# Interleaving the two token halves in the activations, so that stationary operands are read with a step of two columns

## The chip, the cores and the metric

The kernel runs on one core of a Trainium2 chip. The metric is the device time of one execution in microseconds, as the median of several runs. TensorE does the matrix products: a load (LDWEIGHTS) puts a stationary operand of up to 128 x 128 numbers in place, and a matmul then streams a moving operand of up to 512 columns past it and adds the result into an accumulator in PSUM. VectorE and ScalarE work on what comes out, DMA queues bring the weights from memory. Each engine works through its own queue of instructions, and they wait for each other by semaphores.

## The reference

256 tokens with 2048 features go through two transformer-like blocks in float32. What matters here is that nearly all of the work is products of activations with weight matrices:

```python
proj = h @ w_in[i]
...
merged = (jax.nn.sigmoid(gate_sb) * (y_sb @ w_sb_out[i])
          + jax.nn.sigmoid(gate_ca) * (y_ca @ w_ca_out[i]))
x = x + merged @ w_mix_out[i]
h = rmsnorm(x, g_ffn[i])
g_ff, u_ff = jnp.split(h @ w_ffn_in[i], 2, axis=-1)
x = x + (jax.nn.silu(g_ff) * u_ff) @ w_ffn_out[i]
...
x = x + jax.nn.sigmoid(h @ w_ple_gate[i]) * (p[i] @ w_ple_in[i])
```

The first block has two attention branches, a feed-forward part with 5632 hidden features and a gated addition. The second block has a state-space branch, a gated linear attention, a differential attention, and a feed-forward part with 5504 hidden features and a short convolution over the tokens.

## The kernel before

Every float32 operand of a large product is split into a high part in the format fp32r and a low part, the rest. A product is then three products: low by high, high by low and high by high, accumulated in the same place. The weights are split as they arrive (`high`, a cast on ScalarE, L485; `low`, a subtraction on VectorE, L495) into one long tile `W`, some halves ahead of their use.

An activation is held feature-major in an `Acts` object: in slots of [128 features, 4, 512], where the 512 columns of one group of 128 features are first the high parts of tokens 0 to 255 and then their low parts. `at(k)` gives the 512 columns of group k, `two(k)` those of two groups. The splitting is done by `hilo` (L317): ScalarE writes the high part (L320, or L312 with a scale), VectorE the low part (L321, or L315 with a scale). It is called wherever activations are made: at the start from the transposed input, in `to_acts` after TensorE's transposes (L348), in `yt_out` and `head_norm` for the heads of the attentions, in `hidden1` and `hidden2` of the feed-forward parts, in `ple_start`, and at the end of the state-space branch `s5`.

A list of jobs is worked off in order by `stream`; each job is a chain of halves, and a half is one weight transfer of 512 KB. There are two kinds that matter:

- Token-major jobs (`AS`, in `mm_as`): the stationary operand is 128 tokens of an activation's high or low part, the moving operand 512 columns of a weight. For each group of features and each half m of the tokens there are three matmuls: L583 (low activation, high weight), L584 (high activation, low weight), L585 (high, high). Each has a load of its own. The result is [128 tokens, 2 halves, 512].
- Feature-major jobs (`WS`): the stationary operand is a 128 x 128 piece of a weight, the moving operand an activation. L545 streams all 512 columns (high and low tokens) past the weight's high part, L549 the 256 high columns past its low part. The result holds, for 128 output features, 256 columns of one kind and 256 of the other, and `ws_sum` (L441) adds the two: a copy on ScalarE (L444), an addition on VectorE (L445), and where a row norm is to be applied a product on VectorE (L447).

A third kind (`W4`, one job) streams an activation past 32 columns of a weight at a time (L538). The first half of all is worked off with the low weights last (`low_last`, L573 to L576), because they arrive last.

Between the halves, `tick` lets generators advance that issue the work on the other engines, so the order of instructions on each engine is fixed when the kernel is built.

Of the kernel before, what the change touches and what calls it, by code (L numbers as in the profile page):

```python
# [168 lines left out]
class Acts:  # L169


    def __init__(self, n):
        self.n, self.slots, self.ready = n, {}, set()

    def at(self, k):
        return self.slots[k // 4][0][:, k % 4, :]

    def two(self, k):
        return self.slots[k // 4][0][:, k % 4:k % 4 + 2, :]


class Job:
# [5 lines left out]
class Build:  # L188
# [127 lines left out]

    def hilo(self, hi, lo, src, scale=None):  # L317

        if scale is None:
            self.nc.scalar.copy(hi, src)  # L320
            self.nc.vector.tensor_sub(lo, src, hi.bitcast(F32))  # L321
        else:
            self.act(hi, src, AF.Copy, scale=scale)
            self.stt(lo, src, scale, ALU.mult, hi.bitcast(F32), ALU.subtract)


    def open_acts(self, acts, g):
# [11 lines left out]
    def to_acts(self, src, acts, n, scale=None, gcol=None):  # L339

        yield from self.open_acts(acts, n)
        banks = []
        for half in range(2):
            b = yield from self.bank()
            for kk in range(2):
                for m in range(2):
                    c = half * 256 + kk * 128
                    self.nc.tensor.transpose(b[0][:, kk * 256 + m * 128:kk * 256 + m * 128 + 128],  # L348
                                             src[:, m, c:c + 128], self.ident)
            banks.append(b)  # L350
        yield
        for half in range(2):
            k = 4 * n + 2 * half
            if gcol is None:
                t = acts.two(k)
                ps = banks[half][0].rearrange("p (k t) -> p k t", k=2)
                self.hilo(t[:, :, 0:256], t[:, :, 256:512], ps, scale)
            else:
                for kk in range(2):
                    t = acts.at(k + kk)  # L360
                    self.hilo(t[:, 0:256], t[:, 256:512], banks[half][0][:, kk * 256:kk * 256 + 256],
                              self.par[:, gcol + k + kk:gcol + k + kk + 1])
            acts.ready.update((k, k + 1))
            self.unbank(banks[half])
# [76 lines left out]
    def ws_sum(self, acc, out, rb=None, n=2):  # L441

        nc = self.nc
        nc.scalar.copy(out, acc[:, 0:n, 256:512])  # L444
        nc.vector.tensor_add(out, acc[:, 0:n, 0:256], out)  # L445
        if rb is not None:
            nc.vector.tensor_mul(out, out, rb.tile[:, None, :].to_broadcast([128, n, 256]) if n > 1 else  # L447
                                 rb.tile[:, None, :])


    def stream(self, jobs):
# [56 lines left out]
        for i, (j, idx, ks) in enumerate(halves):  # L508
# [23 lines left out]
            if j.kind == "AS":  # L532
                self.mm_as(j.acts, ks, wh, wl, acc, (0, 1), first, end, low_last=i == 0)
            elif j.kind == "W4":

                for k in range(16):
                    p = slice(32 * (k % 4), 32 * (k % 4) + 32)
                    nc.tensor.matmul(acc[p, 0, :], lhsT=wh[:, 32 * k:32 * k + 32],  # L538
                                     rhs=j.acts.at(k).bitcast(F32), start=k < 4, stop=k >= 12)
            else:  # L540
                for kk, k in enumerate(ks):
                    x = j.acts.at(k)
                    for f in range(2):
                        s = slice((kk * 2 + f) * 128, (kk * 2 + f) * 128 + 128)
                        hi = lambda: nc.tensor.matmul(  # L545
                            acc[:, f, :], lhsT=wh[:, s], rhs=x, start=k == first, stop=k == end)
                        if k == first:
                            hi()
                        nc.tensor.matmul(acc[:, f, 256:512], lhsT=wl[:, s], rhs=x[:, 0:256], start=False, stop=False)  # L549
                        if k != first:  # L550
                            hi()
# [10 lines left out]
    def mm_as(self, acts, ks, wh, wl, acc, ms, first, end, low_last=False):  # L562

        nc = self.nc
        if low_last:
            for low in (False, True):
                for kk, k in enumerate(ks):
                    s = slice(kk * 512, kk * 512 + 512)
                    for m in ms:
                        x = acts.at(k)  # L570
                        xh, xl = x[:, m * 128:m * 128 + 128], x[:, 256 + m * 128:384 + m * 128]
                        if low:
                            nc.tensor.matmul(acc[:, m, :], lhsT=xh, rhs=wl[:, s], start=False, stop=False)  # L573
                        else:
                            nc.tensor.matmul(acc[:, m, :], lhsT=xl, rhs=wh[:, s], start=k == first, stop=False)
                            nc.tensor.matmul(acc[:, m, :], lhsT=xh, rhs=wh[:, s], start=False, stop=False)  # L576
            return
        for kk, k in enumerate(ks):
            x = acts.at(k)
            s = slice(kk * 512, kk * 512 + 512)  # L580
            for m in ms:
                xh, xl = x[:, m * 128:m * 128 + 128], x[:, 256 + m * 128:384 + m * 128]
                nc.tensor.matmul(acc[:, m, :], lhsT=xl, rhs=wh[:, s], start=k == first, stop=False)  # L583
                nc.tensor.matmul(acc[:, m, :], lhsT=xh, rhs=wl[:, s], start=False, stop=False)  # L584
                nc.tensor.matmul(acc[:, m, :], lhsT=xh, rhs=wh[:, s], start=False, stop=k == end)  # L585
# [38 lines left out]
    def first(self):  # L624
# [6 lines left out]
        def start(load):  # L631
# [10 lines left out]
            for k in range(16):  # L642
# [4 lines left out]
                    tri = self.more_consts("tri", 256, nc.sync)  # L647
                    self.U, self.msb = tri[:, 0:128], tri[:, 128:256]
                yield from self.open_acts(XT, k // 4)
                t = XT.at(k)  # L650
                self.hilo(t[:, 0:256], t[:, 256:512], xs[k // 8][0][:, k % 8, :], self.col(P_GMIX + k))
                XT.ready.add(k)
                if k % 2:
                    yield
# [41 lines left out]
        def yt_out(Y, h, b, key):  # L696

            yield from self.open_acts(Y, h // 4)
            t = Y.at(h)
            self.hilo(t[:, 0:256], t[:, 256:512], b[0][:, 0:256])  # L700
            Y.ready.add(h)
            self.unbank(b)
            Y.left -= 1
# [157 lines left out]
        def ple_start():  # L861
# [3 lines left out]
            s = self.slot([128, 2, 256])  # L865
            nc.gpsimd.dma_start(out=s[0], in_=d["pt"])
            PT.slots[0] = self.slot([128, 4, 512], F32R)
            t = PT.two(0)
            self.hilo(t[:, :, 0:256], t[:, :, 256:512], s[0])
            self.drop(s)  # L870
            PT.ready.update((0, 1))

# [87 lines left out]
    def hidden1(self, j, kl, acc, free, hid, rb):  # L960
# [8 lines left out]
        self.act(s[:, 0], s[:, 0], AF.Silu)  # L969
        v.tensor_mul(s[:, 0], s[:, 0], s[:, 1])  # L970
        yield
        t = hid.at(kl)
        self.hilo(t[:, 0:256], t[:, 256:512], s[:, 0])
        hid.ready.add(kl)

    def ffn(self, wu, wd, nf, acts, rb, hidden, fin):
# [419 lines left out]
    def head_norm(self, b, t, w, acts, h, post):  # L1396
# [20 lines left out]
        for vh in range(2):  # L1417
# [6 lines left out]
        dst = acts.two(2 * h)  # L1424
        self.hilo(dst[:, :, 0:256], dst[:, :, 256:512], t.rearrange("p (a t) -> p a t", a=2))
        acts.ready.update((2 * h, 2 * h + 1))
        yield

    def hidden2(self, j, kl, acc, free, hid, rb):
# [17 lines left out]
        self.act(c[:, 1], c[:, 1], AF.Silu)  # L1447
        v.tensor_mul(c[:, 0], c[:, 0], c[:, 1])
        yield
        h = hid.at(kl)  # L1450
        self.hilo(h[:, 0:256], h[:, 256:512], c[:, 0])
        hid.ready.add(kl)


# [203 lines left out]
    def s5(self, uslot, ZT):  # L1658
# [61 lines left out]
        for j2 in range(4):  # L1720
# [33 lines left out]
            if j2 % 2:  # L1754
# [5 lines left out]
                t = ZT.slots[g][0]  # L1760
                yield

                for jj in range(4):
                    yt = y[:, jj].rearrange("p (t c) -> p c t", t=4)
                    hi, lo = (t[:, jj, h:h + 256].rearrange("p (c t) -> p c t", t=4) for h in (0, 256))
                    self.hilo(hi, lo, yt)
                    if jj % 2:
                        yield
# [25 lines left out]
```

## Time and profile before

| | |
|---|---|
| median of 3 runs | 3138.79 us (3138.43 to 3139.48) |
| the profiled execution, whole | 3139.36 us |
| its span, from the first to the last instruction | 3137.6 us |
| mean granted TensorE clock | 0.999 |
| data moved by DMA | 618 MB, 197 GB/s in the mean |

The rows of the profile that matter stand in the prediction. A row of a group names the line, the engine, the operation, what it writes and reads, its shape and its count; behind the first bar are the busy time in us and the mean duration of one in ns, behind the second the engine's idle time before such instructions, and what ended it. A row of the timeline begins with the start and the duration in us. PE is TensorE's matmuls, PEld its loads of stationary operands, DVE is VectorE, ACT is ScalarE. Matmuls overlap: a matmul's duration is longer than the distance to the next one's start.

### The profile page before, as it was taken

To read this page: it belongs to the slowest core of one execution; us is meant where nothing else is said; L and a number is where in the kernel's file an instruction comes from. 1 tells how busy PE (TensorE), PEld (TensorE's weight loads), DVE (VectorE), ACT (ScalarE), POOL (GpSimd) and SP (SyncE) were. 2 spreads that over 40 slices of the span, in tenths; PEclk is the share of its full clock that TensorE was granted. 3 is DMA by queue.
4 is the path that set the end of the run, shared out by engine and by line. 5 is a ranking of instruction groups with operands and counts; after the bars stand their busy time and mean duration, and the time that the engine had idled before them with its cause. 6 is when DMAs were issued, how large, how long until landed. Compare 5 with 4: busy or idle time off the path is not lost.

```text
span 3137.6 us, 45166 instructions
## 1 busy us (share of the span) xinstructions
PE 3119.9 (99%) x17629; PEld 2651.4 (85%) x17629; DVE 1993.1 (64%) x2593; ACT 1553.3 (50%) x2035; POOL 73.4 (2%) x158
## 2 busy tenths in 40 slices
PE   9999999999999999999999999999999999999998
PEld 7888888888888888888888888888888888888887
DVE  5656445557577677566655667945555766757766
ACT  6544444455444454456544454444445654545545
POOL 0000000000001000000000001000000000000000
PEclk9999999999999999999999999999999999999999
DMA  7554555555667766655654575655555555555554
GB/s 265 170 180 163 189 194 187 182 189 189 216 224 243 255 224 233 198 175 189 216 181 162 174 221 197 211 191 199 200 186 181 190 195 186 191 196 188 192 188 168
DMA packets 172645, 618.00 MB, mean 197 GB/s; under 512 B 23552, under 2 KB 23968, under 8 KB 169232
## 3 DMA queue, kind: packets, MB, share of 16 engines
q1 hardware_dynamic: 164992, 577.49, 55.4%
q0 software_dynamic: 7440, 37.64, 3.5%
q8 instruction: 138, 2.26, 0.3%
q14 instruction: 75, 0.61, 0.1%
HBM read 599.74 MB, written 14.25 MB: 196 GB/s over the span
## 4 chain that ended last, share of the span: by engine, by line
PE 99%; ACT 0%; DMA 0%; DVE 0%; DVEq 0%; issue 0%; SPq 0%; ACTq 0%
PE acc L545 29%; PE acc L583 17%; PE acc L584 17%; PE acc L585 17%; PE acc L549 15%; PE p L348 1%; PE p L1699 0%; PE p L1739 0%; PE p L1156 0%; PE p L930 0%; PE p L931 0%; PE p L932 0%; PE p L1152 0%; PE p L1742 0%; PE p L1133 0%; PE p L1733 0%
## 5 line engine op out<-in xcount | busy, mean ns | idle before, releaser
L495 DVE TENSOR_TENSOR w<-raw,w 128x1024 fp32r<-128x1024 f32 x1088 | 1320.2, 1220 | 644.2 <-PE acc L584 421.7
L485 ACT CAST w<-raw 128x1024 fp32r<-128x1024 f32 x1088 | 1138.4, 1049 | 1092.4 <-PE acc L585 637.3
L545 PE MATMUL acc<-s,w 128*128 128x512 f32 x3936 | 1369.5, 393 | 0.0
L549 PE MATMUL acc<-s,w 128*128 128x256 f32 x3936 | 1090.4, 282 | 0.0
L583 PE MATMUL acc<-w,s 128*128 128x512 f32 x2372 | 932.4, 393 | 0.8 <-DVE big L1376 0.8
L585 PE MATMUL acc<-w,s 128*128 128x512 f32 x2372 | 923.6, 389 | 0.0
L584 PE MATMUL acc<-w,s 128*128 128x512 f32 x2372 | 923.5, 389 | 0.0
L545 PEld LDWEIGHTS acc<-s,w 128*128 128x128 f32 x3936 | 733.4, 188 | 153.5
L549 PEld LDWEIGHTS acc<-s,w 128*128 128x128 f32 x3936 | 740.2, 188 | 10.4 <-issue 1.0
L583 PEld LDWEIGHTS acc<-w,s 128*128 128x128 f32 x2372 | 445.6, 188 | 93.8 <-issue 1.7
L585 PEld LDWEIGHTS acc<-w,s 128*128 128x128 f32 x2372 | 445.3, 188 | 93.5
L584 PEld LDWEIGHTS acc<-w,s 128*128 128x128 f32 x2372 | 445.7, 188 | 90.9 <-issue 0.5
L445 DVE TENSOR_TENSOR s<-acc,s 128x512 f32<-128x512 f32 (+1 forms) x120 | 82.7, 690 | 263.8 <-ACT s L444 263.7
L444 ACT COPY s<-acc 128x512 f32<-128x512 f32 (+1 forms) x120 | 70.1, 585 | 189.1 <-PE acc L545 186.9
L312 ACT ACTIVATE s<-s 128x256 f32<-128x256 f32 (+4 forms) x175 | 76.6, 443 | 105.1 <-DVE s L315 38.0
L315 DVE SCALAR_TENSOR_TENSOR s<-s,conv 128x256 f32<-128x256 f32 x172 | 79.4, 482 | 3.1
L447 DVE TENSOR_TENSOR s<-s,rb 128x512 f32<-128x512 f32 (+1 forms) x104 | 71.7, 689 | 3.5
L320 ACT CAST s<-s 128x256 fp32r<-128x256 f32 (+1 forms) x104 | 45.7, 443 | 30.1 <-DVE s L970 15.0
L1655 DVE TENSOR_TENSOR s<-s,s 128x1024 f32<-128x1024 f32 x48 | 58.5, 1220 | 0.0
L312 ACT ACTIVATE s<-s,conv 128x256 f32<-128x256 f32 x86 | 47.1, 595 | 22.0 <-DVE s L447 22.0
L321 DVE TENSOR_TENSOR s<-s,s 128x256 fp32r<-128x256 f32 (+1 forms) x104 | 47.6, 460 | 15.8 <-ACT s L320 15.8
L312 ACT ACTIVATE junk<-big 128x512 f32<-128x512 f32 x48 | 30.3, 632 | 50.7 <-DVE big L949 32.4
(265 smaller groups left out, 1007.7 us busy)
## 6 DMA issues: line engine op xcount, KB each, us to landing
raw<-in_w_fin SPq DMA_DIRECT2D x176, 512.0 KB, 4.3
raw<-in_w_up SPq DMA_DIRECT2D x172, 512.0 KB, 4.0
raw<-in_w_fout SPq DMA_DIRECT2D x88, 512.0 KB, 4.3
raw<-in_w_down SPq DMA_DIRECT2D x84, 512.0 KB, 4.2
raw<-in_w_qksb SPq DMA_DIRECT2D x32, 512.0 KB, 3.8
raw<-in_w_qkca SPq DMA_DIRECT2D x32, 512.0 KB, 3.5
raw<-in_w_gsb SPq DMA_DIRECT2D x32, 512.0 KB, 3.9
raw<-in_w_gca SPq DMA_DIRECT2D x32, 512.0 KB, 4.2
```

What stands on the lines that cost most here:

```text
L312: self.nc.scalar.activation(out, in_, func, scale=scale, **kw)
L315: self.nc.vector.scalar_tensor_tensor(out=out, in0=in0, scalar=scalar, in1=in1, op0=op0, op1=op1)
L444: nc.scalar.copy(out, acc[:, 0:n, 256:512])
L445: nc.vector.tensor_add(out, acc[:, 0:n, 0:256], out)
L447: nc.vector.tensor_mul(out, out, rb.tile[:, None, :].to_broadcast([128, n, 256]) if n > 1 else rb.tile[:, None, :])
L485: nc.scalar.copy(wh[:, :n], raws[i][:, :n])
L495: nc.vector.tensor_sub(wl[:, :n], r[:, :n], wh[:, :n].bitcast(F32))
L545: hi = lambda: nc.tensor.matmul(acc[:, f, :], lhsT=wh[:, s], rhs=x, start=k == first, stop=k == end)
L549: nc.tensor.matmul(acc[:, f, 256:512], lhsT=wl[:, s], rhs=x[:, 0:256], start=False, stop=False)
L583: nc.tensor.matmul(acc[:, m, :], lhsT=xl, rhs=wh[:, s], start=k == first, stop=False)
L584: nc.tensor.matmul(acc[:, m, :], lhsT=xh, rhs=wl[:, s], start=False, stop=False)
L585: nc.tensor.matmul(acc[:, m, :], lhsT=xh, rhs=wh[:, s], start=False, stop=k == end)
```

## The change

The 256 tokens are stored so that the two halves take turns: token t of half 0, token t of half 1, token t + 1 of half 0, and so on, first for all high parts, then for all low parts. `at(k)` and `two(k)` give two views now, one of the high and one of the low parts, with the indices half m and token t, in which t steps by two columns. `moving(k)` is new and gives the 512 columns as they lie.

- Token-major matmuls take as stationary operand the 128 tokens of a half from these views, so that each load reads every second column. Moving operand, order and number of matmuls stay.
- Feature-major matmuls and the `W4` job stream `moving(k)`, as they lie. Their results' columns then stand in the alternating order, and `ws_sum` reads the accumulator with a step of two and writes the usual order.
- `hilo` writes its two results through the alternating views. Where it is given a scale and two groups at once (`to_acts` with a constant scale), VectorE's part is done in two instructions, one for each group.
- In `s5` the reordering of the tokens at the end goes through the same views.

```diff
 class Acts:
+    def moving(self, k):
+        return self.slots[k // 4][0][:, k % 4, :]
+
     def at(self, k):
-        return self.slots[k // 4][0][:, k % 4, :]
+        v = self.moving(k).rearrange("p (h t m) -> p h m t", h=2, m=2)
+        return v[:, 0], v[:, 1]
 
     def two(self, k):
-        return self.slots[k // 4][0][:, k % 4:k % 4 + 2, :]
+        v = self.slots[k // 4][0][:, k % 4:k % 4 + 2, :].rearrange("p k (h t m) -> p h k m t", h=2, m=2)
+        return v[:, 0], v[:, 1]
...
     def hilo(self, hi, lo, src, scale=None):
+        if len(src.shape) < len(hi.shape):
+            src = src.rearrange("p (m t) -> p m t" if len(src.shape) == 2 else "p k (m t) -> p k m t", m=2)
         if scale is None:
             self.nc.scalar.copy(hi, src)
             self.nc.vector.tensor_sub(lo, src, hi.bitcast(F32))
         else:
             self.act(hi, src, AF.Copy, scale=scale)
-            self.stt(lo, src, scale, ALU.mult, hi.bitcast(F32), ALU.subtract)
+            for k in range(hi.shape[1]) if len(hi.shape) == 4 else (slice(None),):
+                self.stt(lo[:, k], src[:, k], scale, ALU.mult, hi[:, k].bitcast(F32), ALU.subtract)
...
     def ws_sum(self, acc, out, rb=None, n=2):
-        nc.scalar.copy(out, acc[:, 0:n, 256:512])
-        nc.vector.tensor_add(out, acc[:, 0:n, 0:256], out)
+        a = acc[:, 0:n, :].rearrange("p n (h t m) -> p h n m t", h=2, m=2)
+        o = out.rearrange("p n (m t) -> p n m t", m=2)
+        nc.scalar.copy(o, a[:, 1])
+        nc.vector.tensor_add(o, a[:, 0], o)
...
-                    x = j.acts.at(k)
+                    x = j.acts.moving(k)
...
         for kk, k in enumerate(ks):
-            x = acts.at(k)
             s = slice(kk * 512, kk * 512 + 512)
             for m in ms:
-                xh, xl = x[:, m * 128:m * 128 + 128], x[:, 256 + m * 128:384 + m * 128]
+                xh, xl = (x[:, m] for x in acts.at(k))
                 nc.tensor.matmul(acc[:, m, :], lhsT=xl, rhs=wh[:, s], start=k == first, stop=False)
                 nc.tensor.matmul(acc[:, m, :], lhsT=xh, rhs=wl[:, s], start=False, stop=False)
                 nc.tensor.matmul(acc[:, m, :], lhsT=xh, rhs=wh[:, s], start=False, stop=k == end)
...
-                    yt = y[:, jj].rearrange("p (t c) -> p c t", t=4)
-                    hi, lo = (t[:, jj, h:h + 256].rearrange("p (c t) -> p c t", t=4) for h in (0, 256))
+                    yt = y[:, jj].rearrange("p (t m c) -> p m c t", t=4, m=2)
+                    hi, lo = (t.rearrange("p m (c t) -> p m c t", t=4) for t in ZT.at(4 * g + jj))
                     self.hilo(hi, lo, yt)
```

The other places of the diff are calls of `hilo`, which pass `*acts.at(k)` or `*acts.two(k)` in place of two slices.

More of the change, by code (lines that the diff above doesn't have):

```diff
@@ L356, in to_acts @@
                 ps = banks[half][0].rearrange("p (k t) -> p k t", k=2)
-                self.hilo(t[:, :, 0:256], t[:, :, 256:512], ps, scale)
+                self.hilo(*t, ps, scale)
             else:
@@ L360, in to_acts @@
                     t = acts.at(k + kk)
-                    self.hilo(t[:, 0:256], t[:, 256:512], banks[half][0][:, kk * 256:kk * 256 + 256],
+                    self.hilo(*t, banks[half][0][:, kk * 256:kk * 256 + 256],
                               self.par[:, gcol + k + kk:gcol + k + kk + 1])
@@ L538, in stream @@
                     nc.tensor.matmul(acc[p, 0, :], lhsT=wh[:, 32 * k:32 * k + 32],
-                                     rhs=j.acts.at(k).bitcast(F32), start=k < 4, stop=k >= 12)
+                                     rhs=j.acts.moving(k).bitcast(F32), start=k < 4, stop=k >= 12)
             else:
                 for kk, k in enumerate(ks):
-                    x = j.acts.at(k)
+                    x = j.acts.moving(k)
                     for f in range(2):
@@ L578, in mm_as @@
         for kk, k in enumerate(ks):
-            x = acts.at(k)
             s = slice(kk * 512, kk * 512 + 512)
             for m in ms:
-                xh, xl = x[:, m * 128:m * 128 + 128], x[:, 256 + m * 128:384 + m * 128]
+                xh, xl = (x[:, m] for x in acts.at(k))
                 nc.tensor.matmul(acc[:, m, :], lhsT=xl, rhs=wh[:, s], start=k == first, stop=False)
@@ L649, in start @@
                 yield from self.open_acts(XT, k // 4)
-                t = XT.at(k)
-                self.hilo(t[:, 0:256], t[:, 256:512], xs[k // 8][0][:, k % 8, :], self.col(P_GMIX + k))
+                self.hilo(*XT.at(k), xs[k // 8][0][:, k % 8, :], self.col(P_GMIX + k))
                 XT.ready.add(k)
@@ L698, in yt_out @@
             yield from self.open_acts(Y, h // 4)
-            t = Y.at(h)
-            self.hilo(t[:, 0:256], t[:, 256:512], b[0][:, 0:256])
+            self.hilo(*Y.at(h), b[0][:, 0:256])
             Y.ready.add(h)
@@ L867, in ple_start @@
             PT.slots[0] = self.slot([128, 4, 512], F32R)
-            t = PT.two(0)
-            self.hilo(t[:, :, 0:256], t[:, :, 256:512], s[0])
+            self.hilo(*PT.two(0), s[0])
             self.drop(s)
@@ L971, in hidden1 @@
         yield
-        t = hid.at(kl)
-        self.hilo(t[:, 0:256], t[:, 256:512], s[:, 0])
+        self.hilo(*hid.at(kl), s[:, 0])
         hid.ready.add(kl)
@@ L1423, in head_norm @@
                 self.stt(c, c, s1, ALU.mult, s2, ALU.mult)
-        dst = acts.two(2 * h)
-        self.hilo(dst[:, :, 0:256], dst[:, :, 256:512], t.rearrange("p (a t) -> p a t", a=2))
+        self.hilo(*acts.two(2 * h), t.rearrange("p (a t) -> p a t", a=2))
         acts.ready.update((2 * h, 2 * h + 1))
@@ L1449, in hidden2 @@
         yield
-        h = hid.at(kl)
-        self.hilo(h[:, 0:256], h[:, 256:512], c[:, 0])
+        self.hilo(*hid.at(kl), c[:, 0])
         hid.ready.add(kl)
@@ L1759, in s5 @@
                 yield from self.open_acts(ZT, g)
-                t = ZT.slots[g][0]
                 yield
                 for jj in range(4):
-                    yt = y[:, jj].rearrange("p (t c) -> p c t", t=4)
-                    hi, lo = (t[:, jj, h:h + 256].rearrange("p (c t) -> p c t", t=4) for h in (0, 256))
+                    yt = y[:, jj].rearrange("p (t m c) -> p m c t", t=4, m=2)
+                    hi, lo = (t.rearrange("p m (c t) -> p m c t", t=4) for t in ZT.at(4 * g + jj))
                     self.hilo(hi, lo, yt)
```

## The prediction

> **What bounds the kernel now.** I read the page's head first, then its chain, then the costliest groups, and then the timeline, because the groups' durations overlap and do not say how fast matmuls follow each other.
>
> ```profile
> span 3137.6 us, 45166 instructions
> PE 3119.9 (99%) x17629; PEld 2651.4 (85%) x17629; DVE 1993.1 (64%) x2593; ACT 1553.3 (50%) x2035; POOL 73.4 (2%) x158
> ...
> PE 99%; ACT 0%; DMA 0%; DVE 0%; DVEq 0%; issue 0%; SPq 0%; ACTq 0%
> PE acc L545 29%; PE acc L583 17%; PE acc L584 17%; PE acc L585 17%; PE acc L549 15%; PE p L348 1%; PE p L1699 0%; PE p L1739 0%; PE p L1156 0%; PE p L930 0%; PE p L931 0%; PE p L932 0%; PE p L1152 0%; PE p L1742 0%; PE p L1133 0%; PE p L1733 0%
> ```
>
> TensorE is busy for 99% of the span and is 99% of the chain that ended last. The three token-major lines (L583, L584, L585) are 17% each, so about half the span. The other half is the feature-major pair L545 and L549. The list of TensorE's waits has two entries:
>
> ```profile
> PE acc L575 <- ACT w L485: 7.7, 1, 7.7
> PE acc L583 <- DVE big L1376: 0.8, 1, 0.8
> ```
>
> After the start, TensorE waited 0.8 us for anybody. The time is therefore the number of matmuls times the distance from one start to the next. The counts and the loads of the stationary operand:
>
> ```profile
> L583 PE MATMUL acc<-w,s 128*128 128x512 f32 x2372 | 932.4, 393 | 0.8 <-DVE big L1376 0.8
> L585 PE MATMUL acc<-w,s 128*128 128x512 f32 x2372 | 923.6, 389 | 0.0
> L584 PE MATMUL acc<-w,s 128*128 128x512 f32 x2372 | 923.5, 389 | 0.0
> ...
> L585 PEld LDWEIGHTS acc<-w,s 128*128 128x128 f32 x2372 | 445.3, 188 | 93.5
> ```
>
> There are 3 x 2372 = 7116 token-major matmuls of 512 columns, each with a load of its own that takes 188 ns. Their distance, from TensorE's timeline:
>
> ```profile
> 1450.01 0.39 PE L584 MATMUL acc<-w,s 128*128 128x512 f32 x1
> 1450.23 0.39 PE L585 MATMUL acc<-w,s 128*128 128x512 f32 x1
> ...
> 1455.45 0.39 PE L584 MATMUL acc<-w,s 128*128 128x512 f32 x1
> ```
>
> From one L584 to the eighth L584 after it are 24 matmuls: 5.44 us / 24 = 226.7 ns. What 512 columns need at least is seen at the very start, where TensorE still ran slowly (the granted clock reads 1.00 there, so the pace itself is the sign):
>
> ```profile
> 8.30 0.63 PE L576 MATMUL acc<-w,s 128*128 128x512 f32 x1
> ...
> 10.86 0.63 PE L576 MATMUL acc<-w,s 128*128 128x512 f32 x1
> ```
>
> ```profile
> 7.70:13.00 5.30, 5.29 (x13) 1.00 1.03 409
> ```
>
> Six distances in 2.56 us are 426.7 ns each, which I read as exactly half speed: 2 x 213.3. Then 512 columns cost 213.3 ns at full speed, and each of the 7116 matmuls carries **13.3 ns** that is not columns. In all that is 94.9 us. The feature-major pairs carry the same:
>
> ```profile
> 1502.71 0.39 PE L545 MATMUL acc<-s,w 128*128 128x512 f32 x1
> 1502.94 0.28 PE L549 MATMUL acc<-s,w 128*128 128x256 f32 x1
> ...
> 1504.80 0.39 PE L545 MATMUL acc<-s,w 128*128 128x512 f32 x1
> ```
>
> Six pairs in 2.09 us are 348 ns a pair, to the 10 ns of the view; 512 and 256 columns are 320 ns, so some 14 ns remain for each matmul, whether 512 or 256 columns long. At half speed the extra vanished altogether. A fixed step at each change of the stationary operand would be longer at half speed, or as long. Something that fits into the gaps of a slower stream behaves as seen. The transposes are a second case:
>
> ```profile
> 1431.21 1.04 PE L348 MATMUL p<-cst,big 128*128 128x128 f32 x8
> ...
> L348 PE MATMUL p<-cst,big 128*128 128x128 f32 x128 | 16.6, 272 | 0.0
> ```
>
> The last of eight takes about 0.27 of the 1.04 us, so seven distances are 0.77 us, 110 ns each. That is twice as long per column as in a large matmul (106.7 ns for 128 columns), and the extra is some 3 ns. Here too the stream is slower and the extra small. So the 13.3 ns looks like the load and the moving stream getting in each other's way while both read.
>
> **The change, part by part.** *The load.* It keeps 128 columns and its place behind the previous matmul; only its addresses change, from neighbouring words to every second word. How quickly it reads comes from two load rows:
>
> ```profile
> L1699 PEld LDWEIGHTS p<-s,s 128*32 128x32 f32 x512 | 7.5, 110 | 2.6 <-issue 2.0 <-PE acc L584 0.4 <-PE acc L549 0.3
> ```
>
> 188 - 110 = 78 ns for 96 more columns is 0.81 ns a column, against 0.417 ns a column for the moving stream. So today the load walks through memory at half the stream's pace, and the stream sweeps past it again and again. With a step of two the load walks 8 bytes in 0.81 ns, which is the stream's own pace. If the two disturb each other where they hit the same part of memory, as the shrinking extra suggests, then one push apart is enough and they stay apart. No row shows a stationary operand with a step, so this is bounded from both sides. The best end is that all 13.3 ns go: -94.9 us. The bad end is that the load, which covers 1024 bytes in place of 512, disturbs twice as much: 13.3 becomes 26.7 ns, +94.9 us. I take the value of the transposes' row, the nearest in which a load hardly disturbs: an extra of 3.3 ns, a distance of 216.6 ns, 10.0 ns less. 7116 x 10.0 = **-71.2 us**.
>
> *The splitting into high and low parts, and the sums.* `hilo` now writes every second word, and `ws_sum` reads the accumulator with that step. The nearest rows are the splittings of the state-space branch, which read with a step of 64 words, beside plain ones:
>
> ```profile
> L320 ACT CAST s<-s x4: 647/658/668, 2081.5 to 2084.2; 128x256 fp32r<-128x256 f32 x4
> ```
>
> ```profile
> L320 ACT CAST s<-s x5: 404/408/409, 2908.2 to 2952.7; 128x256 fp32r<-128x256 f32 x5
> ```
>
> ```profile
> L321 DVE TENSOR_TENSOR s<-s,s x4: 618/621/637, 2082.2 to 2085.0; 128x256 fp32r<-128x256 f32 x4
> ```
>
> ```profile
> L321 DVE TENSOR_TENSOR s<-s,s x5: 417/420/425, 2909.2 to 2953.7; 128x256 fp32r<-128x256 f32 x5
> ```
>
> For 256 columns that is +250 ns on ScalarE and +201 ns on VectorE; the lower bound is nothing. I keep the dear end. The sums:
>
> ```profile
> L445 DVE TENSOR_TENSOR s<-acc,s 128x512 f32<-128x512 f32 (+1 forms) x120 | 82.7, 690 | 263.8 <-ACT s L444 263.7
> L444 ACT COPY s<-acc 128x512 f32<-128x512 f32 (+1 forms) x120 | 70.1, 585 | 189.1 <-PE acc L545 186.9
> ```
>
> A sum has 512 columns, so +0.40 us on VectorE and +0.50 us on ScalarE. The tightest place is the second feed-forward's feature-major stretch, in which twelve blocks of 11.1 us (32 pairs of 347 ns) follow each other:
>
> ```profile
> 2453.00:2586.00 133.00, 133.00 (x717) 115.09 (x717) 95.44 (x127) 71.24 (x95) 1.02 (x10) 1.00 0.58 193
> ```
>
> VectorE is busy for 95.4 of 133 us (the columns are TensorE, loads, VectorE, ScalarE, GpSimd). Twelve blocks add at most 12 x 0.60 = 7.2 us there, and 12 x 0.75 = 9 us to ScalarE's 71.2. Both stay under 80%, behind TensorE, which covers them. `to_acts` gets one more VectorE instruction per pair where its scale is a constant (16 in all, under 0.5 us each), also covered. What is not covered is the first matmul, which waits 7.7 us at the start behind two ScalarE splittings: +0.5 us at most. I put +1 us for that and for joins. No DMA is added or moved, and no queue or wait is reordered. If the token-major stages run 4% faster, the weights must come 4% faster; DMA is busy for 0.58 of the stretch above, so that has room.
>
> **Sum.** The profiled execution took 3139.4 us (its span 3137.6 and 1.8 around it; the median of the runs shown is 3138.8, 0.6 less). 3139.4 - 71.2 + 1 = **3069 us**. Its own range goes from 3139.4 - 94.9 = 3044 to half the gain, 3104.
>
> **The rivals.** *Nothing moves: 3139 to 3141.* The 13.3 ns may belong to the hand-over between two stationary operands, whatever the addresses. For it speaks that it is the same in both kinds of job; against it, that it is absent at half speed. [...]
>
> *Slower: about 3235.* The place is the same 7116 loads. If a load takes a slot from the moving stream for each piece of memory that it opens, and not where the two happen to meet, then twice the bytes covered is twice the price: 13.3 more ns, +94.9 us. It decides from the first token-major job on. For it speaks that the extra is so constant; against it, only that the stream seems to have gaps at half speed, which both readings allow. At worst the load also gets as slow per column as the stepped ScalarE splitting (+0.98 ns a column): 188 + 125 = 313 ns. In the pairs a load of 188 ns fits behind a distance of some 120 ns, so it may run about 70 ns past its matmul's start; behind 226.7 ns about 298 ns fit. The distance would be 242 ns and the time about 3249. [...]
>
> *VectorE or ScalarE becomes the bound.* At under 80% of the tightest stretch I give this no chance of its own.
>
> **How the numbers follow.** Faster by the likeliest mechanism 0.52, nothing moves 0.19, slower around 3235 0.22, worse than that 0.07. A measurement of this kernel can tell about 0.2% (6 us) from no change: faster 0.52, same 0.19, slower 0.29. The range goes from 3044 to 3237 us. It must reach the slower case, since leaving that out would leave out 0.29.
>
> **What would show it.** Right: L583 to L585 start 215 to 219 ns apart, their loads stay near 188 ns, the pairs stay at 347 ns, and the sums and splittings on ScalarE and VectorE get longer without a wait of TensorE. Distances of 227 ns mean that nothing moves; 240 ns and more mean the slower rival, with load rows still at 188 ns if it takes slots, and near 300 ns if it is slow itself. New waits of TensorE for VectorE or ScalarE, or pairs that change, would make the working wrong in a place that I put at nothing.

## The result and the profile after

The change makes the kernel slower. The median of three runs is 3187.67 us (3187.60 to 3187.93) against 3138.79 us: a ratio of 1.0156, with a 95% interval from 1.0142 to 1.017. Of thirteen further runs of the kernel before, made beside the first experiments, twelve lay between 3138.45 and 3140.01 us and one, at 8091.52 us, is not compared with anything here. The prediction was 3069 us with a range from 3044 to 3237; the time lies in the range, but the likeliest direction, faster, was wrong.

The head of the page of the changed kernel and its chain of waits (the line numbers have moved: L545 is now L557, L549 is L561, and L583, L584, L585 are L593, L594, L595):

```profile
span 3186.0 us, 45182 instructions
PE 3168.1 (99%) x17629; PEld 2696.3 (85%) x17629; DVE 1995.6 (63%) x2609; ACT 1555.9 (49%) x2035; POOL 72.8 (2%) x158
...
PE acc L557 28%; PE acc L593 18%; PE acc L595 17%; PE acc L594 17%; PE acc L561 15%; PE p L358 1%; PE p L1703 0%; PE p L1743 0%; PE p L1162 0%; PE p L937 0%; PE p L939 0%; PE p L938 0%; PE p L1158 0%; PE p L1746 0%; PE p L1139 0%; PE p L1737 0%
```

The list of TensorE's waits has the same two entries as before:

```profile
PE acc L586 <- ACT w L497: 7.8, 1, 7.8
PE acc L593 <- DVE big L1382: 0.8, 1, 0.8
```

So TensorE still sets the time and waits for nobody new. It has the same 17629 matmuls and is busy 48.2 us longer. Which ones take longer is seen in the groups, first of the kernel before, which the prediction did not show, then of the one after:

```profile
L545 PE MATMUL acc<-s,w 128*128 128x512 f32 x3936 | 1369.5, 393 | 0.0
L549 PE MATMUL acc<-s,w 128*128 128x256 f32 x3936 | 1090.4, 282 | 0.0
```

```profile
L557 PE MATMUL acc<-s,w 128*128 128x512 f32 x3936 | 1369.7, 393 | 0.0
L561 PE MATMUL acc<-s,w 128*128 128x256 f32 x3936 | 1090.5, 282 | 0.0
L593 PE MATMUL acc<-w,s 128*128 128x512 f32 x2372 | 946.5, 399 | 0.8 <-DVE big L1382 0.8
L595 PE MATMUL acc<-w,s 128*128 128x512 f32 x2372 | 937.2, 395 | 0.0
...
L595 PEld LDWEIGHTS acc<-w,s 128*128 128x128 f32 x2372 | 459.9, 194 | 96.6
```

The feature-major pairs are unchanged to 0.2 us in 1369 and 0.1 in 1090. The token-major matmuls are some 6 ns longer each (393 to 399, 389 to 395), and so are their loads (188 to 194). The distance from one matmul to the next is what counts, and it stands in TensorE's timeline:

```profile
1472.34 0.39 PE L595 MATMUL acc<-w,s 128*128 128x512 f32 x1
...
1477.94 0.40 PE L595 MATMUL acc<-w,s 128*128 128x512 f32 x1
```

From one L595 to the eighth after it are 24 matmuls: 5.60 us / 24 = 233.3 ns, where it was 226.7. With 213.3 ns for the columns, the extra of each matmul went from 13.3 to **20.0 ns**. 7116 x 6.67 ns = 47.4 us, which is nearly all of the 48.4 us by which the span grew. (Summed over the whole trace, each matmul from its start to the next one's, the token-major matmuls take 48.5 us more and the feature-major ones 0.2 us.) At the very start, where the pace was read as half speed, the distance is still that of before:

```profile
8.39 0.63 PE L587 MATMUL acc<-w,s 128*128 128x512 f32 x1
...
10.95 0.63 PE L587 MATMUL acc<-w,s 128*128 128x512 f32 x1
```

Six distances in 2.56 us are 426.7 ns each, as before the change: at that pace the stepped load adds nothing.

The work beside TensorE, the splittings from 2900 to 3100 us and the groups of the sums:

```profile
L329 ACT CAST s<-s x12: 417/433/437, 2909.1 to 3098.6; 128x256 fp32r<-128x256 f32 x12
```

```profile
L330 DVE TENSOR_TENSOR s<-s,s x12: 416/418/422, 2910.2 to 3099.6; 128x256 fp32r<-128x256 f32 x12
```

```profile
L457 DVE TENSOR_TENSOR s<-acc,s 128x512 f32<-128x512 f32 (+1 forms) x120 | 82.7, 689 | 265.1 <-ACT s L456 265.1
L456 ACT COPY s<-acc 128x512 f32<-128x512 f32 (+1 forms) x120 | 70.1, 585 | 188.9 <-PE acc L557 186.7
```

A plain splitting was 408 ns on ScalarE and 420 on VectorE. With the step of two it is 433 and 418. The sums, 690 and 585 ns before, are 689 and 585. Of the step nothing is seen there, except 25 ns for a splitting's write on ScalarE. Over the whole span ScalarE is busy 2.6 us longer and VectorE 2.5 us.

### The profile page after: what moved, and what is told of

It reads as the page before. It is cut to its first block, busy times and chain, and to the rows that moved or that the text cites. A ratio compares the mean times of both kernels' runs of the same rounds, so it can differ in the third digit from the quotient of the medians.

```text
span 3186.0 us, 45182 instructions
## 1 busy us (share of the span) xinstructions
PE 3168.1 (99%) x17629; PEld 2696.3 (85%) x17629; DVE 1995.6 (63%) x2609; ACT 1555.9 (49%) x2035; POOL 72.8 (2%) x158
## 4 chain that ended last, share of the span: by engine, by line
PE 99%; ACT 0%; DMA 0%; DVE 0%; DVEq 0%; issue 0%; SPq 0%; ACTq 0%
PE acc L557 28%; PE acc L593 18%; PE acc L595 17%; PE acc L594 17%; PE acc L561 15%; PE p L358 1%; PE p L1703 0%; PE p L1743 0%; PE p L1162 0%; PE p L937 0%; PE p L939 0%; PE p L938 0%; PE p L1158 0%; PE p L1746 0%; PE p L1139 0%; PE p L1737 0%
## 5 line engine op out<-in xcount | busy, mean ns | idle before, releaser
L557 PE MATMUL acc<-s,w 128*128 128x512 f32 x3936 | 1369.7, 393 | 0.0
L561 PE MATMUL acc<-s,w 128*128 128x256 f32 x3936 | 1090.5, 282 | 0.0
L593 PE MATMUL acc<-w,s 128*128 128x512 f32 x2372 | 946.5, 399 | 0.8 <-DVE big L1382 0.8
L595 PE MATMUL acc<-w,s 128*128 128x512 f32 x2372 | 937.2, 395 | 0.0
L594 PE MATMUL acc<-w,s 128*128 128x512 f32 x2372 | 935.8, 395 | 0.0
L557 PEld LDWEIGHTS acc<-s,w 128*128 128x128 f32 x3936 | 733.4, 188 | 153.4
L561 PEld LDWEIGHTS acc<-s,w 128*128 128x128 f32 x3936 | 740.2, 188 | 10.6 <-issue 1.0
L595 PEld LDWEIGHTS acc<-w,s 128*128 128x128 f32 x2372 | 459.9, 194 | 96.6
L593 PEld LDWEIGHTS acc<-w,s 128*128 128x128 f32 x2372 | 461.1, 194 | 93.8 <-issue 1.6
L594 PEld LDWEIGHTS acc<-w,s 128*128 128x128 f32 x2372 | 460.0, 194 | 91.2 <-issue 0.5
```

The costliest lines, as they stand in the source:

```text
L557: hi = lambda: nc.tensor.matmul(acc[:, f, :], lhsT=wh[:, s], rhs=x, start=k == first, stop=k == end)
```

## The experiments

### Load alone, and layout alone

The first two kernels take the change apart. In e1_load_only the kernel before, with its layout, loads the stationary operand with a step of two, so that a half is every second token and the rows of the results stand in another order. The loads thus read from the same places as those of the kernel after.

```diff
-                xh, xl = x[:, m * 128:m * 128 + 128], x[:, 256 + m * 128:384 + m * 128]
+                xh, xl = x[:, m:256:2], x[:, 256 + m:512:2]
```

> The kernel before, in which only the token-major loads read every second column; the columns lie as before, so a load takes the even or the odd columns of the 256 high or low ones, and the token-major products are formed with mixed tokens. Theory that the whole loss is the load: token-major starts are 233.3 ns apart and the time is that of the changed kernel, 3186 to 3189 us. Rival, that the stepped writing of the splittings or the stepped sums cost TensorE something too: the starts are 233.3 ns apart and the time stays under 3183 us. Rival, that the layout as such (the moving operand in alternating order) slows the matmuls: starts at 226.7 ns, about 3139 us.

In e2_layout_only the kernel after keeps its layout, splittings and sums, and loads 128 neighbouring columns.

```diff
-                xh, xl = (x[:, m] for x in acts.at(k))
+                x = acts.moving(k); xh, xl = x[:, m * 128:m * 128 + 128], x[:, 256 + m * 128:384 + m * 128]
```

> The changed kernel with its alternating layout, its stepped splittings and sums, but with token-major loads that read 128 neighbouring columns (64 tokens of each half, so the token-major products have their tokens mixed). Theory that the whole loss is the load: starts 226.7 ns apart, 3138 to 3141 us. Rival, that the stepped work on ScalarE and VectorE or the layout cost something: over 3145 us.

| | us | ratio to before (95%) |
|---|---|---|
| e1_load_only | 3187.79 | 1.0155 (1.0138 to 1.0172) |
| e2_layout_only | 3139.33 | 1.0001 (0.9991 to 1.001) |

The token-major groups of the load alone, and then of the layout alone:

```profile
L583 PE MATMUL acc<-w,s 128*128 128x512 f32 x2372 | 946.6, 399 | 0.8 <-DVE big L1376 0.8
L585 PE MATMUL acc<-w,s 128*128 128x512 f32 x2372 | 937.2, 395 | 0.0
```

```profile
L593 PE MATMUL acc<-w,s 128*128 128x512 f32 x2372 | 932.1, 393 | 0.8 <-DVE big L1382 0.8
L595 PE MATMUL acc<-w,s 128*128 128x512 f32 x2372 | 923.5, 389 | 0.0
```

The first repeats the kernel after, the second the kernel before. The whole loss comes with the addresses of the loads. The layout, the splittings, the sums and the 16 added instructions cost nothing that the measurement sees.

### What about the addresses: step or start

From here on each kernel ran once (ten runs of e2_layout_only lay between 3138.45 and 3139.94 us). The next kernel varies the place of the load job by job. 24 token-major jobs of the feed-forward parts get a start and a step of their own, and a line of their own (L579, L581, ..., L625), so that one run compares 24 places. All three matmuls of a group load the same columns there.

```diff
+    PATTERNS = ((0, 1), (0, 2), (1, 2), (0, 3), (0, 4), (0, 5), (0, 6), (0, 8), (0, 16), ...)
...
+        base, step = self.PATTERNS[p]
...
+        return x[:, base:base + 127 * step + 1:step]
...
+        f = lambda w, a, b: dict(out=acc[:, m, :], lhsT=y, rhs=w[:, s], start=a, stop=b)
```

> The kernel before, in which 24 of the feed-forward parts' token-major jobs take their stationary operand from other columns: twelve with start 0 and steps of 1, 2, 2 (start 1), 3, 4, 5, 6, 8, 16, 15, 10, 12, twelve with step 1 and starts 0, 1, 2, 4, 8, 16, 32, 64, then step 2 with starts 2, 4, 16, and step 7. The products of these jobs are thus of other tokens and groups. Measured is the distance from one matmul to the next in each job (226.7 ns, an extra of 13.3, with step 1; 233.3, an extra of 20.0, with step 2). Theory A, a fixed part and one slot for each 64 bytes that the load covers (6.7 ns + 6.7 ns for each 512 bytes): step 3 240 ns, step 4 247, step 8 273, step 16 327, and the start does not matter. Theory B, a load of single words pays once for standing alone: every step from 2 up gives 233 ns, and the start does not matter. Theory C, the price is paid where load and stream meet in the same part of memory: the distances go up and down with step and start, with some below 226 ns.

The kernel took 3154.83 us (3139.12 before). The mean distances between the starts of a job's matmuls, in ns, by the start and the step of the load in columns of 4 bytes:

| step, from start 0 | 1 | 2 | 3 | 4 | 5 | 6 | 7 | 8 | 10 | 12 | 15 | 16 |
|---|---|---|---|---|---|---|---|---|---|---|---|---|
| distance | 227 | 233.3 | 235.5 | 235.0 | 236.7 | 237.3 | 238.8 | 245.4 | 246.2 | 268.2 | 236.7 | 235.3 |

| start, at step 1 | 0 | 1 | 2 | 4 | 8 | 16 | 32 | 64 |
|---|---|---|---|---|---|---|---|---|
| distance | 227 | 232.4 | 230.7 | 233.3 | 233.3 | 233.3 | 232.4 | 227.1 |

From the trace, line by line: the loads and matmuls of step 1, then the loads of steps 2, 3 and 4, those of step 8 with their matmuls, and step 1 from start 4 (min/median/max in ns, the first and last start in us):

```profile
L579 PEld LDWEIGHTS acc<-w,s x72: 187/188/189, 2553.1 to 2569.2; 128*128 128x128 f32 x72
L579 PE MATMUL acc<-w,s x72: 387/389/398, 2553.3 to 2569.4; 128*128 128x512 f32 x72
```

```profile
L581 PEld LDWEIGHTS acc<-w,s x72: 193/193/194, 2569.4 to 2586.0; 128*128 128x128 f32 x72
```

```profile
L585 PEld LDWEIGHTS acc<-w,s x72: 251/253/253, 2603.0 to 2619.7; 128*128 128x128 f32 x72
```

```profile
L587 PEld LDWEIGHTS acc<-w,s x72: 307/309/311, 2753.4 to 2770.0; 128*128 128x128 f32 x72
```

```profile
L593 PEld LDWEIGHTS acc<-w,s x72: 322/331/333, 2804.4 to 2821.8; 128*128 128x128 f32 x72
L593 PE MATMUL acc<-w,s x72: 404/410/410, 2804.6 to 2822.1; 128*128 128x512 f32 x72
```

```profile
847.69 16.50 PE L609 MATMUL acc<-w,s 128*128 128x512 f32 x70
```

The last row is one of the timeline, in which 70 matmuls stand together: (16.50 - 0.40) / 69 = 233.3 ns. Two things follow. A price for the memory that the load covers does not fit: step 8 covers eight times the bytes of step 1 and adds 18 ns, step 16 covers sixteen times and adds 8 ns. And the step is not needed for the loss at all. A load of 128 neighbouring columns that starts 4, 8 or 16 columns further right pays the same 20.0 ns as the step of two. A start 64 columns further (256 bytes) is as good as none. And no distance lies below the 226.7 ns of the kernel before.

The load itself takes 188, 193, 253 and 309 ns at steps 1 to 4: nearly the same at steps 1 and 2, clearly longer from step 3 on. Beyond that it does not simply grow with the step: 331 ns at step 8, 363 at step 12, but 299 at step 16.

### Relative place: moving either operand

If the place of one operand against the other decides, then moving both alike changes nothing, and moving the weights' view by d acts as moving the load by 64 - d. In e4_starts_of_both the table holds the load's start and the moving operand's shift, at step 1:

```diff
+    PATTERNS = ((3, 1, 0), (6, 1, 0), ..., (4, 1, 4), (8, 1, 8), (16, 1, 16), (32, 1, 32), (0, 1, 4), ..., (0, 1, 60))
...
+        d = self.PATTERNS[p][2] if s.start == 0 else (self.PATTERNS[p][2] or 64) - 64
+        s = slice(s.start + d, s.stop + d)
```

Where the moving operand is shifted, every second group of features gets d - 64 in place of d, to stay inside the same piece of W. The kernel thus relies on a price that repeats after 64 columns, as that of the load did in e3 (227 ns at start 0, 227.1 at start 64).

> The kernel before, in which 24 of the feed-forward parts' token-major jobs read other columns with step 1, so that their products are of other columns. Thirteen have only the stationary operand's start moved (3, 6, 12, 20, 24, 28, 40, 44, 48, 52, 56, 60, 62 columns); four have both operands moved alike (4, 8, 16, 32); seven have only the moving operand moved (4, 8, 16, 32, 48, 56, 60). Theory C1, what counts is how the two operands lie to each other: moved alike they are 227 ns apart again, and moving the streamed operand alone costs as much as moving the stationary one alone (231 to 234 ns). Theory C2, what counts is the stationary operand's own place in memory: moved alike they stay at 231 to 234 ns, and moving the streamed operand alone leaves 227 ns. Theory C3, the streamed operand's own place counts too, as reading that starts off a boundary: both kinds cost.

It took 3147.41 us (3138.95 before). Distances in ns:

| moved by | 4 | 8 | 16 | 32 | 48 | 56 | 60 |
|---|---|---|---|---|---|---|---|
| the load alone | 233.3 | 233.3 | 233.3 | 232.4 | 229.0 | 233.4 | 226.9 |
| the moving operand alone | 231.7 | 233.4 | 228.9 | 233.3 | 233.2 | 233.3 | 233.3 |
| both alike | 231.1 | 227.0 | 227.0 | 227.2 | | | |

(The load's row is completed from the kernel before it.) The timeline of the jobs with both moved by 8, and with the load alone at 40 and at 60:

```profile
831.72 14.45 PE L607 MATMUL acc<-w,s 128*128 128x512 f32 x63
```

```profile
2786.82 15.56 PE L591 MATMUL acc<-w,s 128*128 128x512 f32 x66
```

```profile
3003.65 14.67 PE L601 MATMUL acc<-w,s 128*128 128x512 f32 x64
```

They give 14.06 / 62 = 226.8, 15.17 / 65 = 233.4 and 14.28 / 63 = 226.7 ns. Moving both by 8, 16 or 32 columns restores the price of before, and a shift of the moving operand by 16 costs what a shift of the load by 48 costs (228.9 and 229.0), one by 48 what a load's start of 16 costs (233.2 and 233.3). For moves by multiples of 8 columns it is thus the place of the two operands relative to each other that counts, repeating after 64 columns; the pairs agree to 0.2 ns, except that a shift by 32 has 233.3 where the load's 32 has 232.4. A move of 4 columns breaks the rule (alike 231.1, the moving operand alone 231.7 where the load's 60 has 226.9), though one of 60 keeps it (233.3, as the load's 4). What decides there was not found.

### The same for the step of two

The prediction thought that a step of two could remove the extra. Perhaps it needed only another start. e5_starts_of_step_two has 18 further starts of the load with step 2, and six shifts of the moving operand.

```diff
+    PATTERNS = ((6, 2, 0), (8, 2, 0), (10, 2, 0), (12, 2, 0), (14, 2, 0), (18, 2, 0), ..., (0, 2, 48), (0, 2, 60))
```

> The kernel before, in which 24 of the feed-forward parts' token-major jobs read their stationary operand with step 2: eighteen with starts 6 to 62, six with start 0 and the moving operand moved by 4, 8, 16, 32, 48, 60 columns. Their products are of other columns. The prediction's theory, that load and stream at one pace stay apart once they are apart: some starts come to 218 ns or less. Theory C1: the distances differ by start between 226 and 236 ns, none under 226, and moving the streamed operand is worth as much as moving the stationary one by as much the other way. Theory B: all 233 ns whatever the start.

It took 3147.95 us (3138.95 before). With those of e3_steps_and_starts there are 23 starts: 16, 18 and 28 give 229.9 to 230.1 ns, all others 231.1 to 233.4. The shifts 32 and 48 of the moving operand give 231.4 and 230.0, the other four 233.3 or 233.4. Here too a shift by a multiple of 8 is worth what the load's start at 64 less the shift is worth (32: 231.4 for both; 48 and start 16: 230.0 and 229.9), and a shift by 4 is not (233.3, start 60 has 231.4). The best, start 18, and start 8 in the timeline:

```profile
2770.70 15.57 PE L589 MATMUL acc<-w,s 128*128 128x512 f32 x67
```

```profile
2570.71 14.63 PE L581 MATMUL acc<-w,s 128*128 128x512 f32 x62
```

15.18 / 66 = 230.0 and 14.24 / 61 = 233.4 ns. No place that was tried brings a stepped load of 128 columns to 226.7 ns beside 512 moving columns, let alone lower. The picture of two readers at one pace that stay out of each other's way falls.

### Moving the weights in the whole kernel

From the tables, W lying 16 columns (64 bytes) lower should help the step of two (to 230.0 ns) and harm the kernel before (to 233.3 ns), which has no step anywhere. One number in the spare columns of a small tile ahead of W moves it. By the order in which the kernel makes its pools, the activations' slots lie ahead of that tile and stay, while the other tiles behind it move along with W. e6_step_two_moved is the kernel after, e7_before_moved the kernel before, with the same edit:

```diff
-        self.par = one.tile([128, P_N + 32], F32, tag="par", name="par")[:, 0:P_N]
+        self.par = one.tile([128, P_N + 16], F32, tag="par", name="par")[:, 0:P_N]
```

> The changed kernel with the weights' tile W 16 columns (64 bytes) lower in memory, nothing else. Theory that the relative place of load and stream sets the price: the token-major starts come down from 233.3 to 230.0 ns, as with step 2 and the moving operand moved by 48 in the jobs measured before (which repeats after 64), and 7116 of them save 23 us: 3164 us, if the feature-major pairs stay at 347 ns. Their price can rise by the same rule: by 3.3 ns for each of 7872 matmuls it is 26 us. Rival, that the step alone sets the price: token-major starts stay at 233.3 ns.

> The kernel before with the weights' tile W 16 columns (64 bytes) lower in memory, nothing else; all loads read neighbouring columns. Theory that the relative place sets the price: token-major starts go up from 226.7 to 233.2 ns without any step, +47 us, so 3186 us, with the pairs' share on top (0 to 52 us). Rival, that steps are what costs: 226.7 ns and 3139 us.

The results are 3176.19 us and **3192.07 us**, with 3138.04 us for the kernel before beside them. The timeline of the changed kernel with W moved, and then of the kernel before with W moved:

```profile
1466.03 0.39 PE L594 MATMUL acc<-w,s 128*128 128x512 f32 x1
...
1469.48 0.39 PE L594 MATMUL acc<-w,s 128*128 128x512 f32 x1
```

```profile
1460.20 0.40 PE L585 MATMUL acc<-w,s 128*128 128x512 f32 x1
...
1465.80 0.40 PE L585 MATMUL acc<-w,s 128*128 128x512 f32 x1
```

15 matmuls in 3.45 us are 230.0 ns, and 24 in 5.60 us are 233.3 ns, both as the tables said. The kernel before with W 64 bytes lower is as slow as the change, 1.7% above itself, without a step in any load. The pairs also moved, from 348.2 to 350.3 ns in the mean; there W is the stationary operand and the activation moves. Summed over the trace, each matmul from its start to the next one's, the kernel before with W moved spends 43.9 us more in the token-major matmuls and 8.4 us more in the feature-major ones.

The changed kernel came to 3176.19 us and not to the 3164 that had been worked out for unmoved pairs: its token-major matmuls saved 19.4 us, not 23, and its pairs took 8.3 us more. So moving W wins back less than half of what the stepped load lost in these matmuls.

### Is it paid along the load, or along the stream

If reads of the load took slots from the stream, a load of fewer columns would take fewer. e8_fewer_columns loads 96, 64 or 32 columns in the inner matmuls of the 24 jobs; the first and last matmul of each result keep 128.

```diff
+    PATTERNS = ((0, 1, 128), (0, 1, 96), (0, 1, 64), (0, 1, 32), (0, 2, 128), ..., (16, 2, 64), (16, 2, 32), ...)
...
+        return x[:, base:base + (n - 1) * step + 1:step]
```

> The kernel before, in which 24 of the feed-forward parts' token-major jobs use fewer columns of the stationary operand (128, 96, 64, 32) at several starts and steps; in each such job the matmuls of the first and last feature groups keep 128. The products of the left-out tokens are not formed in the others. Theory D, the load's reads take time from the stream: the extra shrinks with the columns of the load: at step 1 and start 0, 13.3 ns with 128 columns, 10 with 96, 6.7 with 64, 3.3 with 32, and at step 2 20, 15, 10, 5. Theory E, a fixed hand-over for each change of the stationary operand: 13.3 ns with any number of columns.

It took 3147.75 us (3138.04 before). Distances in ns:

| columns loaded | 128 | 96 | 64 | 32 |
|---|---|---|---|---|
| start 0, step 1 | 227 | 230.0 | 230.0 | 231.7 |
| start 4, step 1 | | 233.2 | 233.3 | 231.1 |
| start 0, step 2 | 233.2 | 230.9 | 231.7 | 233.3 |
| start 0, step 8 | | 240.0 | 233.3 | 228.9 |
| start 16, step 2 | | | 226.7 | 230.4 |

The other jobs, with starts 16 and 48 at step 1 and start 0 at step 4, lie between 228.3 and 235.6 ns.

The timeline of 32 columns at step 1, and of 64 columns from start 16 at step 2:

```profile
2603.90 12.44 PE L584 MATMUL acc<-w,s 128*32 128x512 f32 x53
```

```profile
1050.73 12.40 PE L616 MATMUL acc<-w,s 128*64 128x512 f32 x54
```

12.05 / 52 = 231.7 and 12.01 / 53 = 226.6 ns. A load of a quarter of the columns pays more, not a quarter. At step 2 it pays the same 20 ns as the whole load. So the extra is no sum over the load's reads, and it is no fixed step either, since it varies from 13.3 to some 20 ns with the number of columns and the place; both theories that were written down fail. (At step 8 the distance does shrink with the columns, from 245.4 ns at 128, measured in e3, where the load took 331 ns, to 228.9 at 32.)

The last kernel, e9_rest_of_starts_and_shorter_streams, shortens the moving operand of the inner matmuls to 448, 384, 320 or 256 columns, and tries twelve further starts at step 1.

```diff
+    PATTERNS = ((5, 1, 512), (7, 1, 512), (10, 1, 512), ..., (0, 1, 448), (0, 1, 384), ..., (0, 2, 320), (0, 2, 256))
...
+        n = 512 if st or sp else self.PATTERNS[p][2]
+        s = slice(s.start, s.start + n)
```

> The kernel before, in which 24 of the feed-forward parts' token-major jobs are changed. Twelve read their stationary operand with step 1 from the starts 5, 7, 10, 14, 18, 22, 26, 30, 36, 58, 61, 63, so with tokens mixed: if 226.7 ns is the least that any start gives, none comes under 226 ns; a start at 222 ns or less would be a kernel faster than before. Twelve stream fewer columns (448, 384, 320, 256) between the first and last feature groups, at start 0 step 1, start 4 step 1 and start 0 step 2; the products of the columns left out are not formed there. Theory F, the extra is paid at the hand-over from one matmul to the next and does not depend on the length: start 0 gives 200, 173, 147, 120 ns and the other two 207, 180, 153, 127 ns. Theory G, the extra is paid along the stream: it shrinks with the length, at 256 columns to half, so 113 ns and 117 ns.

It took 3102.69 us (3138.04 before), less because of the columns left out. With shorter streams TensorE now and then waits for the splitting of the weights (by the list of waits 2.5 us in the job with 256 columns at step 2, 1.1 and 0.2 us in those with 256 and 320 columns from start 4). So the table leaves out distances more than 24 ns above the time of the columns, which stand at such waits and where other work comes in between; they are at most 6 of the 59 of a job. Taking off 213.3 / 512 ns a column, the extra of each matmul in ns is:

| moving columns | 512 | 448 | 384 | 320 | 256 |
|---|---|---|---|---|---|
| start 0, step 1 | 13.3 | 16.0 | 13.6 | 13.3 | 13.3 |
| start 4, step 1 | 20.0 | 20.0 | 13.5 | 13.6 | 11.8 |
| start 0, step 2 | 20.0 | 16.8 | 13.4 | 13.4 | 13.2 |

The timeline of 256 columns from start 0 at step 1, and of 384 columns at step 2:

```profile
838.47 4.72 PE L609 MATMUL acc<-w,s 128*128 128x256 f32 x38
```

```profile
1187.37 7.96 PE L621 MATMUL acc<-w,s 128*128 128x384 f32 x45
```

With 0.28 and 0.34 us for the last matmul they give 4.44 / 37 = 120.0 and 7.62 / 44 = 173.2 ns, over 106.7 and 160.0 ns of columns. Half the stream, the same 13.3 ns. This also confirms the price of the columns without the slow start: 256 columns more take 226.7 - 120.0 = 106.7 ns, 213.3 for 512. So the extra is paid once for each matmul, and not along the stream. Theory F, one price whatever the length, holds for start 0, apart from 448 columns. For the other two places it fails: from 384 columns down they pay about what start 0 pays. At those lengths a load (188 to 195 ns) takes longer than the distance between two matmuls (118 to 174 ns); whether that is why the place stops counting, no run tells. Of the twelve further starts, 30 also gives 226.7 ns and none gives less.

## Why the prediction was wrong, step by step

- **TensorE sets the time, and the time is distance by count: right.** The span grew by 48.4 us, and 7116 x 6.67 ns account for 47.4 of them.
- **The extra of 13.3 ns as load and stream disturbing each other while both read, and "one push apart is enough and they stay apart": wrong.** This is the step that failed, in sign as well as in size. The stepped load was to lower the extra by 10.0 ns, to 3.3; it rose by 6.67 ns, to 20.0, so that the term of -71.2 us came out as +47.4 us. None of the 23 starts of a stepped load of 128 columns lowered it under 16.6 ns (229.9 - 213.3, beside 512 moving columns). And the extra does not grow with the time in which both read: at steps 1 and 2 it follows neither the load's columns (e8: 19.9 ns with 128 at step 2, 20.0 with 32) nor the stream's (e9: 13.3 ns with 512 and with 256 at step 1), but is paid once for each matmul. That the two operands bear on each other was not wrong, since their relative place counts (e4: 227.0 ns with both moved by 8, 233.3 and 233.4 with one alone); whether they do so at the hand-over from one stationary operand to the next or in the first reads stays open.
- **"At half speed the extra vanished", as the reason against a hand-over: a reading that did not decide.** That the 426.7 ns of the start are columns alone, at half of the later pace, was the author's reading. The stepped load, which later pays 20.0 ns, has the same 426.7 ns there, and the price is one for each matmul all the same. How a hand-over would behave at a slower pace no run shows.
- **"Some 14 ns for each matmul" of the pairs: a mean of two unlike ones.** Over the trace of the kernel before, L545 to L549 is 230.7 ns and L549 to the next L545 118.9 ns, so the extras are some 17 and 12 ns.
- **The transposes' 3.3 ns as the nearest value: misleading.** They stand 110 ns apart for 128 columns, 0.86 ns a column against 0.417 in the large products. That the 3.3 ns are an extra rests on reading this as half the pace, as at the start, and no run shows so small an extra beside 0.417 ns a column: the least found is 11.8 ns for short streams and 13.3 for 512 columns.
- **The rival "nothing moves": half right.** It had a price paid once for each matmul, and lost with the words "whatever the addresses": e7_before_moved is 54 us slower by 64 bytes of placement.
- **The rival "slower, about 3235": right in direction, by another mechanism.** It expected 13.3 more ns for twice the memory covered, and 6.67 were measured. Its own mechanism falls with step 8 and step 16 in e3 (245.4 and 235.3 ns, where eight and sixteen times the memory is covered).
- **Worst case, a load slowed to 313 ns: did not come.** It measured 194 ns; from step 3 on such loads exist (253 and 309 ns).
- **Splittings and sums hidden: right, and far too dear.** The neighbouring rows had a step of 64 words and +250 and +201 ns; with a step of two it is +25 ns on ScalarE and nothing on VectorE, and e2 shows no cost to the time at all.
- **Of the announced signs**, loads near 188 ns, unchanged pairs and no new wait came; longer splittings came on ScalarE alone, and longer sums on neither engine; the distance of 233.3 ns lies between the 227 of "nothing moves" and the 240 of "slower". That 3187.67 us lies inside the range is owed to the rival "slower", for whose sake the range was wide, and not to the working.

So the step of two is hardly slow as a load (194 against 188 ns). It gives up a favourable place, and part of its loss is one of place: of the 6.67 ns, 3.3 could be won back by another start or by moving W (230.0 ns), and 3.3 by nothing that was tried with loads of 128 and streams of 512 columns. At step 1, 33 starts were tried, and the kernel before stands at one of the four (0, 30, 60 and 64) that pay the least price found for 512 columns, 13.3 ns; most others pay 20, as the stepped load does where it is. That place may have been chosen: the tile ahead of W has 32 columns that nothing uses, and e7 took 16 of them away. Why some places pay less, why it repeats after 256 bytes and why 4 columns break the pattern stays open. No version was found that beats the kernel before.

## What to carry to other kernels

Where one engine sets the time with thousands of equal instructions, measure the distance between their starts and compare it with the least that their columns need. Here the rest was 13.3 or 20.0 ns by where the tiles lay, and placement alone made two kernels differ by 1.7%. Before a gain or a loss is credited to an access pattern, run the pattern alone and the placement alone: one kernel each settled here what reasoning from rows had wrong. And that no rest was seen at the start's 426.7 ns did not show here what it is made of.

## What the runs showed of the hardware that was not expected

- The place of the stationary operand relative to the moving one, modulo 64 columns (256 bytes), changes the distance of 512-column matmuls at step 1, from 226.7 to 233.3 ns for nearly all of 33 starts (235.0 at most), at the same load time of 187 to 189 ns. With 384 moving columns and fewer the three places tried differ by less than 2 ns. Moving the weights' tile by 64 bytes cost the kernel before 54 us.
- A load of 32 columns, in the same place, has a larger extra (231.7 ns a matmul) than one of 128 (227 ns).
- A load took nearly the same time at steps 1 and 2 (188, 193 ns) and 253, 309, 331 and 363 ns at steps 3, 4, 8 and 12, yet up to step 4 the distance stays within 235.5 ns.
- A step of two on VectorE costs nothing for 256 columns (420 and 418 ns) or for sums read from PSUM (690 and 689 ns), and on ScalarE 25 ns for 256 columns (408 and 433 ns) and nothing for the sums (585 ns both).
